# Dense part of a hybrid decoder trunk: weight splits off GpSimd, norm squares after the gains, another order of the first loads

## The chip, the cores and the metric

One NeuronCore of a Trainium2 chip runs the whole program. The metric is device time in microseconds for one execution. The kernel before took 1980.95 us (median of 3 runs, 1980.83 to 1982.15).

## What is computed

A causal decoder trunk of two layers for 256 tokens of width 1024, all in float32. Each layer has a token mixer and then a channel mixer, both behind an RMS norm and both added to the residual stream. The core of the reference:

```python
for layer in range(2):
    h = rms_norm(x, norm_mix_g[layer])
    x = x + hybrid_mixer(h, ...)
    h = rms_norm(x, norm_ffn_g[layer])
    x = x + (swiglu(h, ...) if layer == 0 else moe_swiglu(h, ...))
return rms_norm(x, norm_final_g)
```

The mixer projects h to nine blocks of 1024 columns, runs a gated 3-tap convolution, a GLU with a 31-tap depthwise convolution, layer norm and swish, and a trailing-mean pool over 2, 4, 8 and 16 tokens; it projects the three branches, gates and sums them and projects the sum. Layer 0 has a dense SwiGLU of width 3584, layer 1 a top-2-of-8 mixture of such experts.

## The kernel before, in words

**Matmuls.** Activations lie transposed: channels on the 128 partitions, 256 tokens along the row. A float32 product is made of three fp32r matmuls (`mm3`, L192 to L194): weights and activations are each split into a high part h and a low part l, and the kernel adds h*h, h*l and l*h. A `pair` makes 256 output channels: 8 x 2 weight blocks of 128x128, 48 matmuls, one PSUM bank. In the mixers four banks are used in turn.

**Weights.** `Stream` brings them in chunks of 128x2048 (1 MB, 16 blocks, so one pair for one chunk), in the order of use. `load` (L88) issues the transfers on SyncE's queue, at most four raw buffers deep. `split_upto` makes wh by a ScalarE copy (L112) and wl by a subtraction. The subtraction is one VectorE instruction for a whole chunk (L117). For the chunks listed in `shared`, every odd one of both mixers, VectorE takes the first 1024 columns (L114) and GpSimd the other 1024 (L115). Three split buffers let the splits run ahead of TensorE. The very first chunk is loaded in halves and split in quarters.

**Norm.** The norm's scale is known late, so the first six pairs run on x*gain (`xg`), unscaled, and `descale` multiplies their results by the row of 1/rms. `norm_pair(n, j)` handles 256 channels: two ScalarE copies with the gain (L262), two VectorE instructions for the low part (L263), a ScalarE square (L266, L269) and, for j > 0, a GpSimd add into the sum of squares (L270). `norm_rstd` sums over partitions on TensorE (L228) and takes the inverse root in 12 tiny VectorE instructions (L214 to L220); `norm_row` spreads it over tokens (L236, L241).

**Mixer.** Eight pairs make the GLU, then pool, short convolution (L480, L486), gates and projections. The 31-tap convolution, its layer norm and swish run in the background: a generator emits a few of its instructions at each `bg(k)` call. Its products come from ScalarE (L358) or stay on VectorE (L341), the sums from VectorE (L363). The layer norm adds its squares on GpSimd (L398). The last four gates (L496) and the projection of the result follow it.

**Order.** The instructions of each engine run in one fixed order. It is set when the program is built, by a scheduler that plays the program through on a model of the engines and takes, of what is ready, what was written first; an order can be pinned by hand.

**Head.** SyncE's queue issues, in this order: x's first quarter, prm (gains, 52 KB), weight chunk 0 in two halves, x's other quarters, chunk 1, cst, chunks 2 and 3. ScalarE's queue issues lp (the mixer's parameters, 152 KB).

Of the kernel before, what the change touches and what calls it, by code (L numbers as in the profile page):

```python
# [6 lines left out]
F32 = mybir.dt.float32  # L7
# [8 lines left out]
P = 128  # L16
T = 256
D = 1024
KC = D // P
# [16 lines left out]
N_HL2 = 1  # L36
N_PAD = 4
LEAD = 2
H_POOL = (1, 2, 3)
POOL_ON_DVE = (3,)  # L40

# [7 lines left out]
W2_LATE = E * NFC * 6 - 4  # L49
W2_LATE_AT = {(i, j): (W2_LATE + (j // 2 + 2 if j % 2 else i), HALF * (i if j % 2 else j // 2))  # L50
              for i in range(2) for j in range(4)}


N_MIXER = (72 + 3 * 8 + 8) * KC // (CHUNK // P) + 4 * 4 // (CHUNK // P)
N_FFN = 3 * F // P * KC // (CHUNK // P)
MIXER_CHUNKS = [*range(1, N_MIXER), *range(N_MIXER + N_FFN, 2 * N_MIXER + N_FFN)]


K_ID, K_IOTA, K_INV, K_TRI = 0, 128, 256, 320
# [3 lines left out]
class Act:  # L63


    def __init__(self, h, l):
        self.h, self.l = h, l


class Stream:  # L70


    def __init__(self, nc, srcs, raw, hl, shared):
        self.nc, self.hl, self.shared = nc, [hl] * N_HL, shared
        self.chunks = [s[i] for s in srcs for i in range(s.shape[0])]
        self.n = len(self.chunks)
        self.loaded, self.split, self.pos, self.turn = 0, 0, 0, 0
        self.raws, self.hls = {}, {}
        self.free = [raw] * N_RAW

    def load(self, n=None):

        while self.free and self.loaded < self.n and n != 0:
            c, pool = self.loaded, self.free.pop(0)
            t = pool(f"raw{c}")
            w = HALF if c == 0 else HALF // 2 if c == self.n - 1 else CHUNK
            for o in range(0, CHUNK, w):
                self.nc.sync.dma_start(t[:, o:o + w], self.chunks[c][:, o:o + w])  # L88
            self.raws[c] = (t, pool)
            self.loaded += 1  # L90
            n = n if n is None else n - 1
# [5 lines left out]
    def more_split(self, hl, n):  # L97
        self.hl += [hl] * n

    def split_upto(self, upto):  # L100
        nc = self.nc
        while self.split < min(upto, self.n):
            c = self.split
            t, pool = self.raws.pop(c)
            hl = self.hl[self.turn % len(self.hl)]
            self.turn += 1
            h = hl.tile([P, CHUNK], F32R, tag="wh", name=f"wh{c}")
            l = hl.tile([P, CHUNK], F32R, tag="wl", name=f"wl{c}")
            w = CHUNK // 4 if c == 0 or c == self.n - 1 else HALF if c == self.n - 2 else CHUNK
            for o in range(0, CHUNK, w):  # L110
                d = slice(o, o + w)
                nc.scalar.activation(h[:, d], t[:, d], AF.Copy)  # L112
                if c in self.shared:
                    nc.vector.tensor_tensor(l[:, :HALF], t[:, :HALF], h[:, :HALF].bitcast(F32), ALU.subtract)  # L114
                    nc.gpsimd.tensor_tensor(l[:, HALF:], t[:, HALF:], h[:, HALF:].bitcast(F32), ALU.subtract)  # L115
                else:
                    nc.vector.tensor_tensor(l[:, d], t[:, d], h[:, d].bitcast(F32), ALU.subtract)  # L117
            self.hls[c] = (h, l)
            self.split += 1
            self.free.append(pool)  # L120
            self.load()
# [24 lines left out]
def body(ctx, tc, x_in, prm_in, cst_in, wd_in, wm_in, out):  # L146
# [8 lines left out]
    xT = const.tile([P, KC, T], F32, name="xT")  # L155
    cst = const.tile([P, K_TRI], F32, name="cst")
    prm = const.tile([P, C_END], F32, name="prm")
    ws = Stream(nc, [wd_in, wm_in], lambda name: raw.tile([P, CHUNK], F32, tag="raw", name=name), hlp,
                shared=[c for c in MIXER_CHUNKS if c % 2])

    def load_x(j):
        nc.sync.dma_start(xT[:, 2 * j:2 * j + 2, :], x_in[:, 2 * j:2 * j + 2, :])

    load_x(0)
    nc.sync.dma_start(prm, prm_in[:, 0:C_END])
    ws.load(1)
    for j in range(1, 4):
        load_x(j)
    ws.load(1)
    nc.sync.dma_start(cst, cst_in[:, 0:K_TRI])  # L170
    ws.load()

# [4 lines left out]

    warm = const.tile([P, 1], F32, name="warm")
    nc.scalar.activation(warm, ones[:, 0:1], AF.Sigmoid)

    def col(c, t=prm):
        return t[:, c:c + 1]
# [61 lines left out]
    def new_pair(pool, name):  # L244
        return Act(pool.tile([P, KC, T], F32R, tag="pair", name=f"{name}_h", bufs=6),
                   pool.tile([P, KC, T], F32R, tag="pair", name=f"{name}_l", bufs=6))
# [5 lines left out]
        return n  # L252

    def norm_pair(n, j):
        xp = xT[:, 2 * j:2 * j + 2, :]
        if j == 0:
            n.acc = n.pool.tile([P, 2, T], F32, tag="work", name=f"{n.name}_sqa", bufs=3)
            if n.split:
                n.xg = new_pair(n.pool, f"{n.name}_xg")
        if n.split:  # L260
            for k in (2 * j, 2 * j + 1):
                nc.scalar.activation(n.xg.h[:, k, :], xT[:, k, :], AF.Copy, scale=col(n.g + k))  # L262
                nc.vector.scalar_tensor_tensor(n.xg.l[:, k, :], xT[:, k, :], col(n.g + k),  # L263
                                               n.xg.h[:, k, :].bitcast(F32), ALU.mult, ALU.subtract)
        if j == 0:
            nc.scalar.activation(n.acc, xp, AF.Square)  # L266
        else:
            sq = n.pool.tile([P, 2, T], F32, tag="work", name=f"{n.name}_sq{j}", bufs=3)
            nc.scalar.activation(sq, xp, AF.Square)  # L269
            nc.gpsimd.tensor_tensor(n.acc, n.acc, sq, ALU.add)  # L270
# [33 lines left out]
    def mixer(l, n, dp, on_pair, before_out=lambda: None):  # L304
        with ExitStack() as st:
            mp = st.enter_context(tc.tile_pool(name=f"mix{l}", bufs=1))
            lp = mp.tile([P, M_END], F32, name=f"lp{l}")
            nc.scalar.dma_start(lp, prm_in[:, C_END + l * M_END:C_END + (l + 1) * M_END])
            cvp = st.enter_context(tc.tile_pool(name=f"cvp{l}", bufs=1, space=PSUM))
            mm2 = st.enter_context(tc.tile_pool(name=f"mm2_{l}", bufs=1, space=PSUM))  # L310
            banks[:], turn[0] = [mmp] * 3 + [mm2], 0
# [116 lines left out]
            for j in range(4):  # L428
                s = slice(2 * j, 2 * j + 2)
                ps_v = n.pair(pair)  # L430
                if j == 0:
                    norm_row(n)
                ps_g = n.pair(pair)
                v, g = descale(n, ps_v, 2 * j, tmp), descale(n, ps_g, 2 * j + 1, tmp)
                sg = tmp(f"vsg{l}_{j}")
                nc.scalar.activation(sg, g, AF.Sigmoid)
                nc.vector.tensor_tensor(vg[:, s, CFK - 1:], v, sg, ALU.mult)
                if j == 0:
                    norm_scaled(n)
                else:  # L440
                    bg(8)
# [100 lines left out]
    def ffn(n, dp, nxt):  # L542
        with ExitStack() as st:
            fp = st.enter_context(tc.tile_pool(name="ffn", bufs=1))
            ap = st.enter_context(tc.tile_pool(name="facc", bufs=1, space=PSUM))
            accs = [ap.tile([P, 2, T], F32, name=f"facc{i}") for i in range(4)]
            gs = {}

            def down(fs, js):
                for f, k, m in [(f, k, 2 * j + i) for f in fs for k in range(2) for j in js for i in range(2)]:  # L550
                    wh, wl = ws.take(P)
                    mm3(accs[m // 2][:, m % 2, :], wh, wl, gs[f].h[:, k, :], gs[f].l[:, k, :],
                        start=(f == 0 and k == 0 and m % 2 == 0), stop=(f == NFP - 1 and k == 1))

            def tmp(name):
                return fp.tile([P, 2, T], F32, tag="ft", name=name, bufs=6)

            for f in range(NFP):
                ps_a = n.pair(pair)
                if f == 0:  # L560
                    norm_row(n)
                ps_c = n.pair(pair)
                a, c = descale(n, ps_a, 2 * f, tmp), descale(n, ps_c, 2 * f + 1, tmp)
                sg, t = tmp(f"fsg{f}"), tmp(f"ft{f}")
                nc.scalar.activation(sg, a, AF.Silu)
                nc.vector.tensor_tensor(t, c, sg, ALU.mult)
                gs[f] = Act(fp.tile([P, 2, T], F32R, tag="gh", name=f"gh{f}", bufs=3),
                            fp.tile([P, 2, T], F32R, tag="gl", name=f"gl{f}", bufs=3))
                split2(gs[f], slice(0, 2), t)
                if f == 0:  # L570
                    norm_scaled(n)
                if 1 <= f < NFP - 1:
                    down([f - 1], range(4))
            for j in range(4):
                down([NFP - 2, NFP - 1], [j])
                xp = xT[:, 2 * j:2 * j + 2, :]
                nc.vector.tensor_tensor(xp, accs[j], xp, ALU.add)
                norm_pair(nxt, j)


    class Router:
# [385 lines left out]
    class Final:  # L967
# [24 lines left out]
        def finish(self):  # L992
# [3 lines left out]
            for n, j in enumerate(self.used):  # L996
# [6 lines left out]
    dp = ctx.enter_context(tc.tile_pool(name="dense", bufs=1))  # L1003
    norms = [norm_begin(dp, c, f"n{i}", split=(i < 3)) for i, c in
             enumerate((C_G1[0], C_G2[0], C_G1[1], C_G2[1]))]
    for j in range(4):
        norm_pair(norms[0], j)
    norm_rstd(norms[0])
    mixer(0, norms[0], dp, lambda j: norm_pair(norms[1], j))
    norm_rstd(norms[1])  # L1010
    ffn(norms[1], dp, norms[2])
    norm_rstd(norms[2])
    router = Router(norms[3], dp)
    pools = []

# [140 lines left out]
```

## Time and profile before

| what | value |
|---|---|
| median of 3 runs | 1980.95 us |
| the profiled execution's own time | 1979.97 us |
| its span, first to last instruction | 1978.2 us |
| TensorE busy | 96% of the span, mean granted clock 0.981 |
| VectorE, ScalarE, GpSimd busy | 80%, 65%, 12% |

The profiled execution lies 0.98 us under the median, and 1.77 us of it lie outside the span. TensorE is busy almost throughout, so a change shows in the time where it removes or adds idle time of TensorE, or time at half clock. Times in rows count from the start of the span.

### The profile page before, as it was taken

To read this page: it belongs to the slowest core of one execution; us is meant where nothing else is said; L and a number is where in the kernel's file an instruction comes from. 1 tells how busy PE (TensorE), PEld (TensorE's weight loads), DVE (VectorE), ACT (ScalarE), POOL (GpSimd) and SP (SyncE) were. 2 spreads that over 40 slices of the span, in tenths; PEclk is the share of its full clock that TensorE was granted. 3 is DMA by queue.
4 is the path that set the end of the run, shared out by engine and by line. 5 is a ranking of instruction groups with operands and counts; after the bars stand their busy time and mean duration, and the time that the engine had idled before them with its cause. 6 is when DMAs were issued, how large, how long until landed. Compare 5 with 4: busy or idle time off the path is not lost. (4 is left out here: it accounts for less than half of the span.)

```text
span 1978.2 us, 28849 instructions
## 1 busy us (share of the span) xinstructions
PE 1896.0 (96%) x11819; PEld 1699.4 (86%) x11819; DVE 1588.9 (80%) x1397; ACT 1287.1 (65%) x1301; POOL 245.1 (12%) x135
## 2 busy tenths in 40 slices
PE   8999989999999999978999998999999999999997
PEld 7999989999999999977788886888777888778886
DVE  8999767744469998675888887988878888878886
ACT  6975864533448867654677765776756767667773
POOL 4422342100023423421000000000000000000000
PEclk9999989999999999988999999999999999999998
DMA  7445544554545455445899997999987989879990
GB/s 263 171 171 183 186 165 160 182 185 178 191 155 190 172 192 190 176 174 232 321 375 344 351 337 290 359 366 339 362 307 297 385 328 364 329 283 380 342 361 23
DMA packets 72284, 512.14 MB, mean 259 GB/s; under 512 B 8145, under 2 KB 8657, under 8 KB 10449
## 3 DMA queue, kind: packets, MB, share of 16 engines
q1 hardware_dynamic: 71424, 509.33, 69.2%
q8 instruction: 94, 1.54, 0.3%
q10 hardware_dynamic: 720, 0.90, 0.1%
q14 instruction: 46, 0.37, 0.0%
HBM read 509.15 MB, written 1.05 MB: 258 GB/s over the span
## 5 line engine op out<-in xcount | busy, mean ns | idle before, releaser
L112 ACT ACTIVATE wh<-raw 128x2048 fp32r<-128x2048 f32 (+1 forms) x491 | 925.2, 1892 | 542.2 <-PE mm L193 161.0
L117 DVE TENSOR_TENSOR wl<-raw,wh 128x2048 fp32r<-128x2048 f32 (+1 forms) x438 | 983.6, 2258 | 243.2 <-ACT wh L112 237.0
L192 PE MATMUL mm<-n_h_h,wh 128*128 128x256 f32 x1312 | 372.5, 284 | 4.1 <-DVE cx L480 4.1
L193 PE MATMUL mm<-n_h_l,wh 128*128 128x256 f32 x1312 | 372.1, 284 | 0.0
L194 PE MATMUL mm<-n_h_h,wl 128*128 128x256 f32 x1312 | 372.1, 284 | 0.0
L192 PEld LDWEIGHTS mm<-n_h_h,wh 128*128 128x128 f32 x1312 | 252.8, 193 | 4.4 <-DVE cx L480 4.3
L193 PEld LDWEIGHTS mm<-n_h_l,wh 128*128 128x128 f32 x1312 | 252.8, 193 | 0.0
L194 PEld LDWEIGHTS mm<-n_h_h,wl 128*128 128x128 f32 x1312 | 252.6, 193 | 0.0
L115 POOL TENSOR_TENSOR wl<-raw,wh 128x1024 fp32r<-128x1024 f32 x53 | 149.7, 2824 | 507.6 <-ACT wh L112 500.1
L193 PE MATMUL y<-wl,gt 128*128 128x512 f32 (+1 forms) x464 | 180.7, 392 | 5.2 <-DVE wl L117 5.1
L193 PE MATMUL c<-wl,xe_h 128*128 128x512 f32 x448 | 177.1, 395 | 5.1 <-DVE wl L117 5.1
L193 PE MATMUL a<-wl,xe_h 128*128 128x512 f32 x448 | 178.7, 399 | 3.2 <-DVE wl L117 3.2
L192 PE MATMUL c<-wh,xe_h 128*128 128x512 f32 x448 | 177.1, 395 | 4.9 <-ACT wh L112 4.2
L192 PE MATMUL a<-wh,xe_h 128*128 128x512 f32 x448 | 179.5, 402 | 0.0
L194 PE MATMUL y<-wh,gt 128*128 128x512 f32 (+1 forms) x464 | 178.8, 391 | 0.4 <-DVE gt L871 0.4
L194 PE MATMUL a<-wh,xe_l 128*128 128x512 f32 x448 | 176.8, 396 | 0.0
L194 PE MATMUL c<-wh,xe_l 128*128 128x512 f32 x448 | 176.1, 393 | 0.0
L192 PE MATMUL y<-wh,gt 128*128 128x512 f32 (+1 forms) x464 | 169.7, 391 | 4.9 <-ACT wh L112 4.9
L358 ACT ACTIVATE cvp<-vg,lp 128x256 f32<-128x256 f32 x360 | 153.1, 498 | 20.9 <-DVE cvw L363 19.8
L363 DVE TENSOR_TENSOR cvw<-cvw,cvp 128x1024 f32<-128x1024 f32 (+1 forms) x116 | 110.9, 956 | 3.5 <-ACT cvp L358 1.4
L193 PEld LDWEIGHTS y<-wl,gt 128*128 128x128 f32 x464 | 88.1, 190 | 25.7 <-DVE wl L117 6.9
L192 PEld LDWEIGHTS y<-wh,gt 128*128 128x128 f32 x464 | 88.0, 190 | 24.5 <-ACT wh L112 5.6
(242 smaller groups left out, 3236.3 us busy)
## 6 DMA issues: line engine op xcount, KB each, us to landing
raw<-wm_dram SPq DMA_DIRECT2D x335, 1024.0 KB, 6.7
raw<-wd_dram SPq DMA_DIRECT2D x147, 1024.0 KB, 4.9
xT<-x_dram SPq DMA_DIRECT2D x4, 256.0 KB, 6.8
raw<-wd_dram SPq DMA_DIRECT2D x2, 512.0 KB, 5.8
raw<-wm_dram SPq DMA_DIRECT2D x4, 256.0 KB, 6.3
out_dram<-o SPq DMA_DIRECT2D x2, 256.0 KB, 2.4
out_dram<-o ACTq DMA_DIRECT2D x2, 256.0 KB, 2.4
lp<-prm_dram ACTq DMA_DIRECT2D x2, 152.0 KB, 3.4
```

Source lines behind the costliest of these rows:

```text
L112: nc.scalar.activation(h[:, d], t[:, d], AF.Copy)
L115: nc.gpsimd.tensor_tensor(l[:, HALF:], t[:, HALF:], h[:, HALF:].bitcast(F32), ALU.subtract)
L117: nc.vector.tensor_tensor(l[:, d], t[:, d], h[:, d].bitcast(F32), ALU.subtract)
L192: nc.tensor.matmul(ps, lh, rh, start=start, stop=False, skip_group_check=True)
L193: nc.tensor.matmul(ps, lh, rl, start=False, stop=False, skip_group_check=True)
L194: nc.tensor.matmul(ps, ll, rh, start=False, stop=stop, skip_group_check=True)
L358: nc.scalar.activation(pr[:, i, :], src, AF.Copy, scale=w)
L363: nc.vector.tensor_tensor(dst, acc_c, pr, ALU.add)
```

## The change

Six edits, in the dense part and the head:

1. `shared` goes: every low part of a weight is made by VectorE alone, in one instruction.
2. x comes in one transfer on SyncE's queue; prm goes to ScalarE's queue; chunk 1 too is loaded and split in halves; the mixer's lp in layer 0 goes to SyncE's queue, behind the first chunks.
3. 14 float32 matmuls of a 128x128 block of ones run at the start of TensorE's program; nobody reads them.
4. The first chunk's quarters are pinned: gain copies of pair j, low parts of pair j, split of quarter j, for j = 0 to 3.
5. The squares of the first norm are issued behind the last quarter's copy on ScalarE; those of the norm between the layers come after the gains of all four pairs.
6. `norm_rstd` of the two mixer norms is written after the mixer's first pair, `norm_row` after its second.

```diff
+N_BUSY = 14
...
-            w = HALF if c == 0 else HALF // 2 if c == self.n - 1 else CHUNK
+            w = HALF if c < 2 else HALF // 2 if c == self.n - 1 else CHUNK
...
-            w = CHUNK // 4 if c == 0 or c == self.n - 1 else HALF if c == self.n - 2 else CHUNK
+            w = CHUNK // 4 if c in (0, self.n - 1) else HALF if c in (1, self.n - 2) else CHUNK
             for o in range(0, CHUNK, w):
                 d = slice(o, o + w)
-                nc.scalar.activation(h[:, d], t[:, d], AF.Copy)
-                if c in self.shared:
-                    nc.vector.tensor_tensor(l[:, :HALF], t[:, :HALF], h[:, :HALF].bitcast(F32), ALU.subtract)
-                    nc.gpsimd.tensor_tensor(l[:, HALF:], t[:, HALF:], h[:, HALF:].bitcast(F32), ALU.subtract)
-                else:
-                    nc.vector.tensor_tensor(l[:, d], t[:, d], h[:, d].bitcast(F32), ALU.subtract)
+                first(o // w)
+                self.last = keep(nc.scalar.activation(h[:, d], t[:, d], AF.Copy))
+                keep(nc.vector.tensor_tensor(l[:, d], t[:, d], h[:, d].bitcast(F32), ALU.subtract))
...
-    load_x(0)
-    nc.sync.dma_start(prm, prm_in[:, 0:C_END])
-    ws.load(1)
-    for j in range(1, 4):
-        load_x(j)
-    ws.load(1)
+    nc.scalar.dma_start(prm, prm_in[:, 0:C_END])
+    nc.sync.dma_start(xT, x_in)
+    ws.load(2)
     nc.sync.dma_start(cst, cst_in[:, 0:K_TRI])
...
+    busy = stp.tile([P, P], F32, tag="st", name="busy")
+    for _ in range(N_BUSY):
+        tc.keep_in_program_order(nc.tensor.matmul(busy, ones, ones, start=True, stop=True))
...
-            nc.scalar.dma_start(lp, prm_in[:, C_END + l * M_END:C_END + (l + 1) * M_END])
+            (nc.scalar if l else nc.sync).dma_start(lp, prm_in[:, C_END + l * M_END:C_END + (l + 1) * M_END])
...
                 ps_v = n.pair(pair)
                 if j == 0:
+                    norm_rstd(n)
+                ps_g = n.pair(pair)
+                if j == 0:
                     norm_row(n)
-                ps_g = n.pair(pair)
...
                 nc.vector.tensor_tensor(xp, accs[j], xp, ALU.add)
-                norm_pair(nxt, j)
+                norm_gain(nxt, j)
+            for j in range(4):
+                norm_square(nxt, j)
...
-    for j in range(4):
-        norm_pair(norms[0], j)
-    norm_rstd(norms[0])
+    keep = tc.keep_in_program_order
+    ws.split_upto(1, lambda q: norm_gain(norms[0], q, keep), keep)
+    with tc.issue_after(ws.last.ins):
+        for j in range(4):
+            norm_square(norms[0], j)
     mixer(0, norms[0], dp, lambda j: norm_pair(norms[1], j))
     norm_rstd(norms[1])
     ffn(norms[1], dp, norms[2])
-    norm_rstd(norms[2])
```

`norm_gain` and `norm_square` are the two halves of `norm_pair`, with the same instructions.

## Rows read from the trace of the kernel before

**Rows 1.** Waits of TensorE (line waited for: us in total, times, longest)

```profile
PE mm L192 <- ACT g L496: 16.8, 2, 8.8
PE mm L192 <- ACT wh L112: 7.8, 1, 7.8
...
PE mm L192 <- DVE cx L480: 4.1, 1, 4.1
...
PE mm L193 <- DVE n_xg_l L263: 2.6, 4, 1.5
...
PE ln_row L236 <- DVE ln_y L220: 1.4, 1, 1.4
PE n_sum L228 <- DVE n_sqa L225: 1.3, 1, 1.3
PE mm L194 <- DVE wl L117: 1.2, 1, 1.2
```

**Rows 2.** Windows: us, busy (instructions) of PE, PEld, DVE, ACT, POOL, granted clock, DMA

```profile
121.40:128.20 6.80, 4.59 (x21) 4.59 (x22) 6.80 (x10) 5.20 (x10) 0.25 (x2) 0.50 0.53 194
...
285.20:295.50 10.30, 5.02 (x22) 4.78 (x23) 7.39 (x8) 9.78 (x17) 3.39 (x1) 0.50 0.30 102
...
7.70:12.10 4.40, 4.33 (x19) 4.11 (x20) 4.20 (x7) 4.29 (x11) 1.20 (x1) 1.00 1.05 399
...
19.00:22.40 3.40, 3.37 (x15) 3.07 (x15) 3.12 (x10) 1.81 (x1) 1.51 (x1) 0.50 0.74 246
22.40:30.00 7.60, 7.60 (x66) 7.60 (x65) 6.17 (x7) 2.30 (x2) 0.86 (x1) 1.00 0.58 212
...
851.80:862.10 10.30, 4.91 (x23) 4.91 (x24) 4.48 (x8) 10.30 (x22) 0.43 (x2) 0.50 0.48 196
```

**Rows 3.** Timeline (start, us, engine, line): the head, and one row of the end

```profile
7.08 2.41 ACT L112 ACTIVATE wh<-raw 128x512 fp32r<-128x512 f32 x4 [0.41 <-DMA raw<-wd_dram]
...
10.72 0.90 ACT L262 ACTIVATE n_xg_h<-xT,prm 128x256 fp32r<-128x256 f32 x2
...
11.52 0.61 ACT L269 ACTIVATE n_sq<-xT 128x512 f32<-128x512 f32 x1
...
1970.15 1.22 PE L236 MATMUL fin_row<-cst,fin_y 128*128 128x128 f32 x4 [2.42 <-DVE fin_y L220]
```

**Rows 4.** VectorE's groups from 30 to 124 us (count, busy us, mean ns)

```profile
L114 DVE TENSOR_TENSOR wl<-raw,wh 128x1024 fp32r<-128x1024 f32 x8 | 16.1, 2013 | 0.0
...
L486 DVE SCALAR_TENSOR_TENSOR c<-cx,lp,c 128x256 f32<-128x256 f32 x4 | 3.8, 994 | 0.0
...
L457 DVE TENSOR_TENSOR us<-us 128x514 f32<-128x514 f32 x1 | 2.3, 2327 | 0.0
...
L457 DVE TENSOR_TENSOR us<-u 128x542 f32<-128x542 f32 x1 | 2.0, 1981 | 0.0
...
L457 DVE TENSOR_TENSOR us<-us 128x538 f32<-128x538 f32 x1 | 0.7, 705 | 0.0
```

**Rows 5.** Line 114, whole span (duration ns min/median/max)

```profile
L114 DVE TENSOR_TENSOR wl<-raw,wh x53: 1206/1227/3465, 18.2 to 887.5; 128x1024 fp32r<-128x1024 f32 x53
```

**Rows 6.** Timeline of VectorE and GpSimd, 113 to 122 us

```profile
113.75 0.87 DVE L486 SCALAR_TENSOR_TENSOR c<-cx,lp,c 128x256 f32<-128x256 f32 x2
...
118.87 2.96 DVE L486 SCALAR_TENSOR_TENSOR c<-cx,lp,c 128x256 f32<-128x256 f32 x2
...
119.05 2.50 POOL L115 TENSOR_TENSOR wl<-raw,wh 128x1024 fp32r<-128x1024 f32 x1 [2.54 <-ACT wh L112]
```

**Rows 7.** Timeline of VectorE and GpSimd, 260 to 273 us

```profile
266.21 2.29 DVE L117 TENSOR_TENSOR wl<-raw,wh 128x2048 fp32r<-128x2048 f32 x1 [2.21 <-ACT wh L112]
...
272.22 3.28 DVE L114 TENSOR_TENSOR wl<-raw,wh 128x1024 fp32r<-128x1024 f32 x1
...
260.50 2.42 POOL L115 TENSOR_TENSOR wl<-raw,wh 128x1024 fp32r<-128x1024 f32 x1 [8.44 <-ACT wh L112]
...
265.12 5.71 POOL L398 TENSOR_TENSOR vsum<-vsum,lsq 128x512 f32<-128x512 f32 x3
```

**Rows 8.** Timeline of VectorE, 584 to 591 us

```profile
584.07 6.88 DVE L263 SCALAR_TENSOR_TENSOR n_xg_l<-xT,prm,n_xg_h 128x256 fp32r<-128x256 f32 x4
```

More of the change, by code (lines that the diff above doesn't have):

```diff
@@ L51 @@
               for i in range(2) for j in range(4)}
-N_MIXER = (72 + 3 * 8 + 8) * KC // (CHUNK // P) + 4 * 4 // (CHUNK // P)
-N_FFN = 3 * F // P * KC // (CHUNK // P)
-MIXER_CHUNKS = [*range(1, N_MIXER), *range(N_MIXER + N_FFN, 2 * N_MIXER + N_FFN)]
 K_ID, K_IOTA, K_INV, K_TRI = 0, 128, 256, 320
@@ L70, with __init__ @@
 class Stream:
-    def __init__(self, nc, srcs, raw, hl, shared):
-        self.nc, self.hl, self.shared = nc, [hl] * N_HL, shared
+    def __init__(self, nc, srcs, raw, hl):
+        self.nc, self.hl = nc, [hl] * N_HL
         self.chunks = [s[i] for s in srcs for i in range(s.shape[0])]
@@ L98, in more_split, with split_upto @@
         self.hl += [hl] * n
-    def split_upto(self, upto):
+    def split_upto(self, upto, first=lambda q: None, keep=lambda ins: ins):
         nc = self.nc
@@ L157, in body @@
     prm = const.tile([P, C_END], F32, name="prm")
[L158 to L162, printed above, removed]
-    load_x(0)
-    nc.sync.dma_start(prm, prm_in[:, 0:C_END])
-    ws.load(1)
-    for j in range(1, 4):
-        load_x(j)
-    ws.load(1)
+    ws = Stream(nc, [wd_in, wm_in], lambda name: raw.tile([P, CHUNK], F32, tag="raw", name=name), hlp)
+    nc.scalar.dma_start(prm, prm_in[:, 0:C_END])
+    nc.sync.dma_start(xT, x_in)
+    ws.load(2)
     nc.sync.dma_start(cst, cst_in[:, 0:K_TRI])
@@ L254, in norm_pair, with norm_gain, norm_square @@
     def norm_pair(n, j):
+        norm_gain(n, j)
+        norm_square(n, j)
+    def norm_gain(n, j, keep=lambda ins: ins):
+        if not n.split:
+            return
+        if j == 0:
+            n.xg = new_pair(n.pool, f"{n.name}_xg")
+        for k in (2 * j, 2 * j + 1):
+            keep(nc.scalar.activation(n.xg.h[:, k, :], xT[:, k, :], AF.Copy, scale=col(n.g + k)))
+            keep(nc.vector.scalar_tensor_tensor(n.xg.l[:, k, :], xT[:, k, :], col(n.g + k),
+                                                n.xg.h[:, k, :].bitcast(F32), ALU.mult, ALU.subtract))
+    def norm_square(n, j):
         xp = xT[:, 2 * j:2 * j + 2, :]
@@ L257, in norm_pair @@
             n.acc = n.pool.tile([P, 2, T], F32, tag="work", name=f"{n.name}_sqa", bufs=3)
[L258 to L265, printed above, removed]
             nc.scalar.activation(n.acc, xp, AF.Square)
@@ L431, in mixer @@
                 if j == 0:
+                    norm_rstd(n)
+                ps_g = n.pair(pair)
+                if j == 0:
                     norm_row(n)
-                ps_g = n.pair(pair)
                 v, g = descale(n, ps_v, 2 * j, tmp), descale(n, ps_g, 2 * j + 1, tmp)
```

## Prediction, made before the change was run

> **What bounds the kernel now.** TensorE is busy nearly all the time, so I first read what it waited for [rows 1]. Seven entries matter: 7.8 us before the first matmul; in the head and at the norm between the layers n_xg_l (four waits, 2.6 us), wl (1.2) and n_sum (1.3); 4.1 us for cx in layer 0's mixer; and, at the end of each mixer, a gate's ScalarE copy (16.8 us in two waits, the longer 8.8, so the other 8.0), with 1.4 us for ln_row. Then I read windows [rows 2], to see what such a wait costs afterwards. From 22.4 us on 66 matmuls start in 7.6 us, 0.12 us each: the engine's full rate. After the cx wait the granted clock is 0.50 for 6.8 us, after each mixer's last wait for 10.3 us; at that level (1.2 of 2.4 GHz) half of a stretch is lost: 3.4 us and twice 5.1 us. So cx stands for 4.1 + 3.4 = 7.5 us, the first mixer's end for 8.0 + 5.1 = 13.1, the second's for 1.4 + 8.8 + 5.1 = 15.3. The time can fall only where these do. The last thing read was why VectorE is late there: its groups, then it and GpSimd side by side [rows 4 to 7].
>
> **No weight splits on GpSimd.** Removed are 53 half splits on GpSimd; VectorE's 53 halves become whole. A half takes 1.21 us when nothing hinders it [rows 5], a whole 2.29 [rows 7], so each costs VectorE 1.08 us. What it gives back: while GpSimd runs a split of 2.50 us, two VectorE instructions that took 0.87 us earlier take 2.96 [rows 6]. From 30 to 124 us, where VectorE has hardly a pause and the cx wait arises, there are 8 halves: 8 x 1.08 = 8.6 us added. Given back [rows 4]: the halves themselves, 8 x (2.01 - 1.21) = 6.4; two of L457, (2.33 + 1.98) - 2 x 0.70 = 2.9; L486, 4 x 0.99 less 2 x 0.87 = 2.2 [rows 4, 6]. That is 11.5, a net relief of 2.9 us, and 0 if a part was due to other GpSimd work; blocked instructions not counted here could make it 5. The cx wait of 4.1 us therefore shrinks to about 1 or goes; a wait of that size (ln_row's 1.4, say) is not one of those followed by half clock in rows 2. **Gain 6 us** of the 7.5; what is late next is ScalarE's copies for the same convolution.
>
> **Ends of the mixers.** The last gates and the projection wait for the layer norm's chain: GpSimd's sum of squares, the inverse root, swish. In the chain of layer 0 a split (2.42 us from 260.50) stands ahead of the three squares' adds, which take 5.71 us [rows 7]; it goes. Then a half of 3.28 us stands before the inverse root; as a whole without GpSimd beside it, it takes 2.29: 1.0 saved. The chain is thus up to 3.4 us shorter. Against this, ScalarE's order (two weight copies and the swish ahead of the gates) is unchanged, and a whole split late in the chain costs 1.1 more. Bounds: 1 us worse, or all 13.1 gone. I take 3 us of wait and about 1 us of half clock: **4 us**. The second mixer's end shows the same wait in rows 1, so the same **4 us**, ln_row's wait among them.
>
> **Norm between the layers.** Four L263, 0.45 us each where nothing hinders them, took 6.88 us beside GpSimd's adds of squares [rows 8]. With gains first, squares and adds come later. The waits there are two of n_xg_l, 2.0 us, and wl, 1.2 [rows 1]. The first go; the second shrinks by a square ahead of its copy, 0.61 less overlap [rows 3], some 0.5. **Gain 2.5 us**, bounds 0 and 3.2. The later squares delay norm_row, but four PSUM banks give TensorE two more pairs, over 11 us, before it needs a bank. Writing norm_rstd and norm_row one pair later costs nothing under the same cover.
>
> **Head.** Lost so far after the first matmul: from 7.7 to 12.1 us 19 matmuls start in 4.4 us; at 0.12 each that is 2.1 us lost. Waits: 0.6 (n_xg_l, the other 2.0 of its 2.6 being the later norm's) and 1.3 (n_sum). Half clock from 19.0 to 22.4: 15 matmuls in 3.4 us, 1.6 lost [rows 1, 2]. Sum 5.6. Lost afterwards: ahead of the first half chunk go 52 + 1024 KB, where 256 + 52 + 152 KB went: 616 KB more, at the 399 GB/s of that window [rows 2] 1.6 us, though longer rows of x may save some; 1.4. The halves of chunk 0 land at about 8.5 and 9.8 us instead of 7.1 [rows 3]. Each quarter takes ScalarE 0.90 + 0.60 us against TensorE's 12 x 0.12 = 1.44: 0.2 in all. Then four squares, 4 x 0.61 = 2.4 us [rows 3], stand ahead of chunk 1's first half copy, about 1.0; the last quarter gives TensorE some 2.1 us of cover: 1.3 idle, and 0.9 for the half's low part. Half clock after that: nothing or 1.6, 0.8 taken. Sum 4.6. **Gain 1 us**, bounds -1.5 (adds of squares hold the low part) and 4 (x lands fast, or the copy goes ahead of the squares).
>
> The 14 matmuls of ones are not in the trace. The nearest row is two float32 products of this size in four pieces, 1.22 us at half clock [rows 3]: 14 x 0.61 = 8.5 us as the upper bound, 14 x 0.305 = 4.3 (the same at full clock) as the lower. They need only the ones, so I start them at 1 us; they end between 5.3 and 9.5. I take 7, at half clock first and full later, and so nothing on the path. If they end early, the idle time behind them may bring half clock back; that is the lower bound above. lp now queues on SyncE behind the chunks, and behind the wait for a free raw buffer; it is needed only with the first tap, tens of microseconds later: nothing. prm takes lp's slot on ScalarE's queue: nothing.
>
> **Sum.** 6 + 4 + 4 + 2.5 + 1 = 17.5 us. The profiled execution, 1979.97 us, would become 1962.5; the median lies 1.0 above it: 1963.5, say 1963.
>
> **Rivals.**
>
> *VectorE becomes the bound.* If what blocked it was GpSimd's other work (adds, pooling), nothing comes back, and the 8.6 us add to the cx wait: 12.7 us, with 10.3 us at half clock instead of 6.8, 1.7 more. That is +10.3; less 3.5 from head and norm, 1988 us. It decides once the relief per split is under 1.08 us. For it: VectorE has no slack there. Against it: 11.5 us over 8 splits are 1.4 each, and rows 6 show the blocking beside a split. Chance 0.10.
>
> *GpSimd's chain is held instead.* Rows 6 show one engine waiting for the whole of the other's instruction; it works both ways, since three adds took 5.71 us [rows 7], 1.9 each. Whole splits of 2.29 us would hold the remaining adds of squares as the half splits of GpSimd delayed them, and the mixers' ends keep their waits: no gain of 4 + 4, perhaps 1 us lost; 1980.95 - 9.5 + 1 = 1972.5. Chance 0.17. The Trainium skill's page "SBUF — State Buffer", section "Who interferes with whom", states this: a VectorE instruction with two SBUF inputs and a GpSimd instruction that reads SBUF exclude one another, and whichever starts first keeps the port for all of its length. By that rule the longer VectorE instruction is the worse holder. The rows agree on the blocking; none shows a whole split holding an add in the chain.
>
> *The order undoes it.* The scheduler's new order keeps the late cx and the late gates: only 3.5 us from head and norm remain, 1977.5, or none. Chance 0.07.
>
> **Numbers.** The forecast has 0.66, its own range 1950 to 1972: the mixers' ends each from 1 worse to 9 better, the head from -1.5 to 4, cx 4 to 7.5. The range for 8 in 10 takes in the second rival and the edge of the third: 1948 to 1977. Outside 0.2%, 4 us, which is about what a measurement of this kernel can tell from no change: faster 0.83 (the forecast and the second rival), within it 0.07, slower 0.10.
>
> **What would show it.** Right: L114 and L115 are gone; L117 takes 2.29 us throughout, L486 0.47; the wait for cx is under 1.5 us and no half clock stands near 120 us; the waits for L496 sum to 8 to 13 us instead of 16.8; n_xg_l leaves the list at the second norm. In the head the first matmul of a weight starts near 9.2 us at full clock, and TensorE's next idle time is before chunk 1. Wrong: a cx wait over 4 us (first rival), L398 still over 1.9 us on average and L496 still at 16 us (second), or the head reaching chunk 2 later than before.

## The result and the profile after the change

The changed kernel is **slower**, by 1.4%: 2009.2 us (median of 4 runs, 2007.83 to 2013.51) against 1981.48 (4 runs of the kernel before beside it), ratio 1.0142, 95% interval 1.013 to 1.0154. The profiled execution took 2008.27 us, its span 2006.4. The prediction was 1963 us, range 1948 to 1977.

First the waits of TensorE in the changed kernel (line waited for: us in total, times, longest), against [rows 1].

```profile
PE mu L382 <- DVE sums L380: 17.5, 2, 9.7
PE mm L183 <- ACT g L495: 14.5, 2, 7.3
PE ln_sum L219 <- DVE vsum L216: 14.0, 2, 7.0
...
PE ln_row L227 <- DVE ln_y L211: 5.0, 2, 2.5
...
PE mm L185 <- DVE wl L111: 3.7, 4, 1.2
```

The cx wait of 4.1 us and the n_xg_l waits are gone, as forecast. But mu and ln_sum, which did not wait before, now wait 17.5 and 14.0 us, twice each: the layer norm at the end of both mixers. Its first wait is for `sums`, the sum over channels that closes the 31-tap convolution.

To see where the time came from, the first of the three matmuls of every weight block was numbered, and its start compared with that of the same number before:

| place | start before, us | after less before, us |
|---|---|---|
| first weight matmul | 7.8 | +0.8 |
| chunk 1 | 18.8 | -2.7 |
| behind the cx wait, chunk 18 | 127.6 | -9.1 |
| last gates, first mixer | 279.1 | -9.5 |
| first mixer's last projection | 290.5 | +10.4 |
| second norm | 589.9 | +8.3 |
| second mixer's last projection | 857.2 | +27.0 |
| end | 1978.2 | +28.2 |

So the change won 9.5 us up to the last gates, and lost 19.9 and 18.7 us at the two mixers' ends. Of the 9.5 us, 1.3 are only put off: the matmuls of mu, ln_sum and ln_row, which the kernel before had run by then. A new wait of 0.95 us for a whole split's wl, at 175 us, had taken 1.2 us back. The timeline of TensorE shows the first end (start us, us, engine, line; in brackets the idle time before and its releaser).

```profile
280.70 1.22 PE L382 MATMUL mu<-sums,ones 128*128 128x256 f32 x2 [7.74 <-DVE sums L380]
288.93 1.01 PE L219 MATMUL ln_sum<-ones,vsum 128*128 128x1 f32 x4 [7.01 <-DVE vsum L216]
292.46 1.19 PE L227 MATMUL ln_row<-cst,ln_y 128*128 128x128 f32 x4 [2.52 <-DVE ln_y L211]
300.91 0.58 PE L183 MATMUL mm<-v_h,wh 128*128 128x256 f32 x1 [7.26 <-ACT g L495]
```

The whole chain from `sums` to the projection's first operand runs with no gate left beside it: 24.5 us idle (7.74 + 7.01 + 2.52 + 7.26), where the kernel before idled 8.0. The windows say what the clock adds and how the stretches compare (us, busy (instructions) of PE, PEld, DVE, ACT, POOL, granted clock, DMA), against [rows 2].

```profile
8.70:12.10 3.40, 3.35 (x15) 3.06 (x16) 3.40 (x8) 3.40 (x9) 0.00 (x0) 0.51 1.05 419
...
52.00:175.40 123.40, 122.55 (x1022) 122.35 (x1020) 115.82 (x129) 98.36 (x163) 13.76 (x16) 1.00 0.49 171
...
210.50:279.40 68.90, 62.46 (x521) 62.25 (x519) 51.68 (x48) 47.55 (x74) 6.48 (x5) 0.97 0.52 183
275.00:305.70 30.70, 8.22 (x32) 7.15 (x33) 15.97 (x32) 16.36 (x35) 3.85 (x3) 0.50 0.11 39
858.70:889.40 30.70, 8.62 (x34) 7.55 (x35) 15.29 (x34) 17.05 (x35) 4.29 (x5) 0.50 0.19 71
```

Half clock now lasts 30.7 us at each end, where it lasted 10.3. Only work that is done at half clock loses time: half of the 8.22 us of PE, 4.1, against half of 5.02, 2.5 [rows 2]. First end: 24.5 - 8.0 in waits and 4.1 - 2.5 in clock are 18.1 of the 19.9 us; the matmuls put off make it 19.4. Second end: 26.5 idle (9.72 + 7.01 + 2.52 + 7.26) less 10.2, and 4.3 - 2.5: 18.1 of 18.7.

**Why `sums` is late.** The line that closes the convolution, in the kernel before and then in the changed one (duration ns min/median/max, then first and last start: one per mixer).

```profile
L383 DVE TENSOR_TENSOR sums<-sums x2: 424/425/426, 252.8 to 822.6; 128x256 f32<-128x256 f32 x2
```
```profile
L380 DVE TENSOR_TENSOR sums<-sums x2: 425/426/426, 280.2 to 863.5; 128x256 f32<-128x256 f32 x2
```

It starts 27.4 us later, though the matmuls beside it are 8.2 us earlier. The convolution works on eight groups of 128 channels, numbered 0 to 7. VectorE's wide adds for groups 0 to 3 end 15.5 us later (their last starts at 175.36, before at 159.90); up to there VectorE is busy 115.8 of 123.4 us, so added work delays them. The last adds, for groups 6 and 7, take 12.4 us longer: from 214.4 to its end at 279.4, before from 199.5 to 252.1. Two chunks of this last stretch on VectorE, first before, then after:

```profile
225.42 1.32 DVE L114 TENSOR_TENSOR wl<-raw,wh 128x1024 fp32r<-128x1024 f32 x1 [0.53 <-ACT wh L112]
226.66 1.49 DVE L363 TENSOR_TENSOR cvw<-cvw,cvp 128x512 f32<-128x512 f32 x2
228.33 1.50 DVE L363 TENSOR_TENSOR cvw<-cvw,cvp 128x512 f32<-128x512 f32 x2 [0.17 <-ACT cvp L358]
231.23 2.29 DVE L117 TENSOR_TENSOR wl<-raw,wh 128x2048 fp32r<-128x2048 f32 x1 [1.40 <-ACT wh L112]
233.44 1.50 DVE L363 TENSOR_TENSOR cvw<-cvw,cvp 128x512 f32<-128x512 f32 x2
...
235.72 0.69 DVE L363 TENSOR_TENSOR cvw<-cvw,cvp 128x512 f32<-128x512 f32 x1
```
```profile
240.26 2.40 DVE L111 TENSOR_TENSOR wl<-raw,wh 128x2048 fp32r<-128x2048 f32 x1 [0.53 <-ACT wh L110]
242.58 1.49 DVE L360 TENSOR_TENSOR cvw<-cvw,cvp 128x512 f32<-128x512 f32 x2
244.25 0.70 DVE L360 TENSOR_TENSOR cvw<-cvw,cvp 128x512 f32<-128x512 f32 x1 [0.17 <-ACT cvp L355]
246.05 2.29 DVE L111 TENSOR_TENSOR wl<-raw,wh 128x2048 fp32r<-128x2048 f32 x1 [1.10 <-ACT wh L110]
248.26 0.69 DVE L360 TENSOR_TENSOR cvw<-cvw,cvp 128x512 f32<-128x512 f32 x1
...
250.57 0.69 DVE L360 TENSOR_TENSOR cvw<-cvw,cvp 128x512 f32<-128x512 f32 x1
```

Each shows 11.5 us, two chunks. Before, seven adds of the convolution fit between the splits; now five. The split that was half grew from 1.32 to 2.40 us. VectorE still pauses (1.10 for wh), but no add could fill this pause. The one after it, at 248.26, needs products that ScalarE makes only from 246.40 on, behind the weight copy for which the split waits too:

```profile
243.30 0.91 ACT L355 ACTIVATE cvp<-vg,lp 128x256 f32<-128x256 f32 x2 [1.47 <-DVE cvw L360]
244.12 1.90 ACT L110 ACTIVATE wh<-raw 128x2048 fp32r<-128x2048 f32 x1
...
246.40 1.70 ACT L355 ACTIVATE cvp<-vg,lp 128x256 f32<-128x256 f32 x4
```

Of the twelve pauses before a split in this stretch (12.6 us together), none had the next add's operands ready. ScalarE in turn had waited 1.47 us for VectorE's add, which stood behind the split of 2.40 us, to free one of the two product buffers. So here the longer split does not only use VectorE's time: it also holds the products back.

### The profile page after: what moved, and what is told of

It reads as the page before. It is cut to its first block, busy times and chain, and to the rows that moved or that the text cites. A ratio compares the mean times of both kernels' runs of the same rounds, so it can differ in the third digit from the quotient of the medians.

```text
span 2006.4 us, 28788 instructions
## 1 busy us (share of the span) xinstructions
PE 1900.8 (95%) x11847; PEld 1703.4 (85%) x11847; DVE 1583.9 (79%) x1398; ACT 1286.1 (64%) x1302; POOL 94.0 (5%) x82
## 5 line engine op out<-in xcount | busy, mean ns | idle before, releaser
L111 DVE TENSOR_TENSOR wl<-raw,wh 128x2048 fp32r<-128x2048 f32 (+1 forms) x492 | 1112.7, 2273 | 269.4 <-ACT wh L110 266.7
L183 PEld LDWEIGHTS y<-wh,gt 128*128 128x128 f32 x464 | 88.0, 190 | 24.5 <-ACT wh L110 5.6
L184 PEld LDWEIGHTS c<-wl,xe_h 128*128 128x128 f32 x448 | 84.6, 189 | 26.7 <-DVE wl L111 8.9
```

What stands on the lines that cost most here:

```text
L111: keep(nc.vector.tensor_tensor(l[:, d], t[:, d], h[:, d].bitcast(F32), ALU.subtract))
L183: nc.tensor.matmul(ps, lh, rh, start=start, stop=False, skip_group_check=True)
L184: nc.tensor.matmul(ps, lh, rl, start=False, stop=False, skip_group_check=True)
```

## The experiments

The theory after the result: whole splits take from VectorE the time in which it did the background convolution; this ends behind the last gates, and the layer norm's chain is exposed. Rivals: GpSimd's part of the chain is at fault, or the new order of norm and head. Runs with a ratio and an interval are medians of four or five executions; the others are single ones. Edits are against the changed kernel unless said otherwise.

**Splits back.** The split by halves returns for all odd mixer chunks but the first.

```diff
+SHARED = [c for c in MIXER_CHUNKS if c % 2 and c > 1]
...
+                if c in SHARED:
+                    nc.vector.tensor_tensor(l[:, :HALF], t[:, :HALF], h[:, :HALF].bitcast(F32), ALU.subtract)
+                    nc.gpsimd.tensor_tensor(l[:, HALF:], t[:, HALF:], h[:, HALF:].bitcast(F32), ALU.subtract)
+                    continue
```

> The changed kernel with the GpSimd half splits put back for the odd mixer chunks from 3 on; all other edits stay. Theory A (the longer VectorE splits make the background convolution late, so that the layer norm's sum mu comes after the last gates): mu's wait on VectorE goes, both mixer ends return to about the waits of before (8 to 9 us and 10 us of half clock each), the gain of the head (2.7 us) and of the second norm (2 us) stay, the cx wait returns at least in part: 1970 to 1978 us. Theory B (the other edits, above all the later norm_rstd and norm_row, start the convolution late): no change, about 2008 us.

Measured: 1974.39 us, ratio 0.9959 (0.9944 to 0.9973). `sums` is back at 250.3 us and the ends wait as before, 8.03 and 1.44 + 8.79 us. The head is 3.7 us ahead by chunk 1, but a half clock from 18.0 us on leaves 0.7 of this by chunk 18; of the cx wait 1.98 us are left; the n_xg_l waits at the second norm are back (1.52 and 0.45).

**The kernel before, without splits on GpSimd** (an edit to the kernel before).

```diff
-                shared=[c for c in MIXER_CHUNKS if c % 2])
+                shared=[])
```

> The kernel before with an empty list of shared chunks; nothing else changed. Theory A: the cx wait goes (6 us gained) and each mixer end loses 15 to 20 us: 2005 to 2016 us. Theory B: only the gain of the cx wait, 1973 to 1976 us.

Measured: 2007.64 us (1999.35 to 2008.45), ratio 1.0114 (1.009 to 1.0138). Its waits of TensorE:

```profile
PE mm L192 <- ACT g L496: 14.5, 2, 7.3
PE ln_sum L228 <- DVE vsum L225: 14.0, 2, 7.0
PE mu L385 <- DVE sums L383: 13.8, 2, 7.7
...
PE ln_row L236 <- DVE ln_y L220: 5.0, 2, 2.5
```

The same four waits, with the old head and the old order of the norm: the splits alone make the loss. The cx gain (6.2 us) and the second norm's (2.2) come with them too, so the second comes from the splits and not from putting the squares last. Even 1.9 us in the head come with them, by chunk 18.

**A shorter convolution**, twice. First 10 of 31 taps are left out for groups 6 and 7 (the last stretch), then 15 of 31 for groups 4 and 5, which VectorE makes alone, long before the end. (The expectations say 11 and 16, but the last tap stays, so each edit leaves out one fewer, and the second 30 instructions of VectorE, not 32.)

```diff
-                    for k in range(CFK):
+                    for k in (range(CFK) if n > 2 else [*range(CFK - 11), CFK - 1]):
```

> The changed kernel with 11 of the 31 taps left out for the last two groups of 128 channels of the convolution (another result for 256 of its channels); all splits stay on VectorE. Theory A: what counts is when the convolution ends against the last gate; 11 rounds at 2.8 rounds per chunk bring mu forward by 4 chunks (22 us), its wait goes, and the two mixer ends fall back to 8 to 13 us of idle time in all each: 1965 to 1980 us. Rival (the chain behind mu is itself longer without GpSimd's halves, whenever it starts): the waits for ln_sum, ln_row and v stay as long, and only mu's own 8 to 10 us go: about 1990 us.

Measured: 1970.02 us. `sums` comes at 257.3 us; of the four waits only ln_row's 1.46 and the projection's 8.78 are left at each end, as at the second end of the kernel before.

```diff
-                    for k in range(CFK):
+                    for k in [*range(CFK - 16), CFK - 1]:
```

> The changed kernel with 16 of the 31 taps left out for the two groups of 128 channels whose taps VectorE makes alone (another result for 256 channels): 32 instructions of about 0.4 us, 13 us of VectorE work less ahead of the last group; all splits stay on VectorE. Leftover theory (the convolution gets what the splits and the foreground leave of VectorE, about 2.5 us per chunk, so 13 us of work are about 5 chunks, 25 to 30 us of its end): the waits for mu and ln_sum go, 1966 to 1976 us. Rival (a microsecond of work is a microsecond of delay): mu comes only 13 us earlier, some waits stay, 1982 to 1992 us.

Measured: 1964.05 us. The line of `sums` in this kernel:

```profile
L380 DVE TENSOR_TENSOR sums<-sums x2: 416/416/417, 251.0 to 812.5; 128x256 f32<-128x256 f32 x2
```

It is 29 us earlier, and mu, ln_sum and ln_row no longer wait. Work taken from VectorE early in the mixer, about 13 us by the expectation's estimate, brings the end forward by more than twice as much: the convolution lives on what VectorE leaves over, long before its last stretch.

**Splits in one part of the mixer**: the first experiment with another list of chunks, early (odd chunks 3 to 27) and late (29 to 41).

```diff
-SHARED = [c for c in MIXER_CHUNKS if c % 2 and c > 1]
+SHARED = [c for c in MIXER_CHUNKS if c % 2 and 1 < c % (N_MIXER + N_FFN) < 28]
```

> The changed kernel with GpSimd's half splits only for the odd chunks 3 to 27 of each mixer, where VectorE has hardly a pause, and none in the later part of the convolution or its layer norm. If the late start of the last convolution group is what costs (VectorE load before it), it comes back: mixer ends as before, 1970 to 1980 us. If the slower rounds of that last group cost as much (2.8 rounds per chunk instead of 3.4, about 13 us), half of the loss stays: 1988 to 1998 us.

```diff
-SHARED = [c for c in MIXER_CHUNKS if c % 2 and c > 1]
+SHARED = [c for c in MIXER_CHUNKS if c % 2 and 28 < c % (N_MIXER + N_FFN) < 42]
```

> The changed kernel with GpSimd's half splits only for the odd chunks 29 to 41 of each mixer, the counterpart of e8_splits_early. If the two stretches simply add up (e8 gave back 20 of 34 us against e1_splits_back), this one gives back about 14 us: 1992 to 1998 us, with the last convolution group starting near 214 us as in the changed kernel. If the last group's rounds are what counts, it gives back more than half: under 1990 us.

Measured: 1988.14 and 1985.05 us. Of the 34.8 us between the changed kernel and the one with all splits back, early splits bring back 21.1 and late ones 24.2, each more than half; the two do not add up. Early, a cx wait of 1.99 us is back; late, the gains at cx and at the second norm stay (9.2 us by the last gates, 2.2 at the norm).

**No splits at the very end** (the first experiment's list without chunks 43, 45 and 47 of each mixer), for the forecast term that GpSimd's splits lengthen the chain.

```diff
-SHARED = [c for c in MIXER_CHUNKS if c % 2 and c > 1]
+SHARED = [c for c in MIXER_CHUNKS if c % 2 and c > 1 and not 40 < (c - 1) % (N_MIXER + N_FFN) < 47]
```

> As e1_splits_back, but no GpSimd split for the chunks 43, 45 and 47 of each mixer, the ones beside the layer norm's chain. The prediction's term (the chain gets 3.4 us shorter without the splits in it): each mixer end loses 3 us of wait and up to 3 us of half clock, 1974 - 10 = 1964 us. Rival (the chain is paced by ScalarE's fixed order and by the chunks, and a whole split on VectorE costs what GpSimd's half cost): within 3 us of e1_splits_back, 1972 to 1977 us.

Measured: 1975.03 us, ratio 0.996 (0.9946 to 0.9974), as with them. The first end still waits 8.29 us, and the three adds of squares on GpSimd still take 5.67: one of them takes 3.12 us, beside a whole split on VectorE.

```profile
L405 POOL TENSOR_TENSOR vsum<-vsum,lsq x6: 1189/1194/3124, 261.0 to 831.3; 128x512 f32<-128x512 f32 x6
```

At the second end ln_row's wait goes and the other is 7.27 instead of 8.79. Measured by the start of the second mixer's last projection, this kernel is 5.4 us ahead of the one with the splits back, of which 1.9 were there at the second norm, so this end won 3.5 us. None of the 5.4 us is left at the kernel's end: with nearly the same waits, TensorE runs 37.5 us at half clock in the expert stage (the mixture of layer 1) behind that projection, and in the kernel with the splits back 23.9. One stretch of it, first splits back, then this kernel:

```profile
1190.00:1260.00 70.00, 63.48 (x282) 50.97 (x281) 58.02 (x44) 45.66 (x34) 0.00 (x0) 0.98 0.80 299
```
```profile
1190.00:1260.00 70.00, 63.47 (x271) 50.86 (x270) 55.70 (x43) 42.85 (x32) 0.00 (x0) 0.93 0.77 295
```

**A third product buffer** for the convolution, and 20 matmuls of ones instead of 14; first on the kernel of the last experiment, then on the changed kernel without any split on GpSimd, then with splits in odd chunks 19 to 41.

```diff
-N_BUSY = 14
+N_BUSY = 20
...
-                            pr = mp.tile([P, 4, T], F32, tag="cvpr", name=f"cvp{l}_{j}_{k}", bufs=2)[:, 0:n, :]
+                            pr = mp.tile([P, 4, T], F32, tag="cvpr", name=f"cvp{l}_{j}_{k}", bufs=3)[:, 0:n, :]
```

> As e4_tail_without, with three buffers instead of two for the convolution's products and 20 instead of 14 matmuls of ones. Theory A (the time hangs on where the convolution's end stands against the last gates): the order has the sum mu about one chunk earlier, so the waits at the mixer ends shrink by 3 to 6 us each and the half clock with them; the ones bridge the 2.1 us of idle time before the first weight matmul, so its chunk runs at full clock, 1 to 2 us: 1955 to 1965 us. Rival: the ends are held by ScalarE's own 8 us of swish and gates, and nothing moves but the head, 1971 to 1974 us.

Measured: **1966.94 us** (1965.23 to 1968.76), ratio 0.9922 (0.9906 to 0.9939), the best of those that make every tap, and better than both kernels. Its waits of TensorE from 100 to 320 us:

```profile
PE mm L193 <- ACT g L505: 3.1, 1, 3.1
PE mm L193 <- DVE cx L489: 2.0, 1, 2.0
```

Against the kernel of the last experiment it is 1.3 us ahead by chunk 18 (the ones) and 6.2 behind the first end (the buffer too). There `sums` is ready only 1.6 us earlier, but mu's matmul starts 5.3 us earlier (248.2 against 253.5): it has a fixed place in TensorE's order, and that place moved.

> The changed kernel with three product buffers (cvpr) instead of two and 20 matmuls of ones instead of 14, no splits on GpSimd. The written order is the same at the convolution's end (mu at place 2164 of TensorE's order, as without the third buffer). Theory (the order of VectorE's work is fixed when the kernel is built, and a third buffer gives VectorE no more time): four waits at each mixer's end of 20 us or more together, as in the changed kernel; only the head changes: no half clock between the ones and the 19th matmul, 1 to 2 us won; total 2005 to 2009. Rival (VectorE's adds wait for ScalarE's products, so the lack of a buffer makes the convolution late): the end waits shrink by 5 us or more each, total under 1998.

Measured: 2000.84 us (one run), between the two expectations. The waits of TensorE from 100 to 320 us:

```profile
PE ln_sum L219 <- DVE vsum L216: 8.8, 1, 8.8
PE mm L183 <- ACT g L495: 7.3, 1, 7.3
PE ln_row L227 <- DVE ln_y L211: 2.5, 1, 2.5
PE mu L382 <- DVE sums L380: 1.1, 1, 1.1
```

A buffer brings `sums` forward by 5.9 us and takes most of mu's wait, part of which ln_sum gets back. So VectorE's adds are also held by the buffers of ScalarE's products, which the theory had denied; it remains the smaller part, since 19.7 us of waits stay where the kernel before had 8.0.

> The changed kernel with the shared splits back for the odd mixer chunks 19 to 41 only, three product buffers (cvpr) instead of two, and 20 matmuls of ones instead of 14. Theory (what VectorE leaves for the convolution decides): the early chunks stay without GpSimd's splits, so the cx wait stays under 1.5 us and about 9 us are won by chunk 19; from there the halves give VectorE back about 0.5 us a chunk, so mu stands at place 2042 of TensorE's fixed order instead of 2164 (the fast version with splits nearly throughout: 1929), and each mixer's end costs 0 to 6 us instead of 19; the second norm keeps its 2 us. Total 1964 to 1972 us. Rival (the splits hurt wherever they stand beside the convolution, and only their removal everywhere or nowhere pays): above 1975, with a wait at the mixers' ends as in the changed kernel.

Measured: 1971.4 us (1970.94 to 1972.86), ratio 0.9953 (0.9937 to 0.997). It keeps the gain at cx (9.2 us by chunk 18) and at the second norm, but waits 0.4 + 9.8 us at each end, more than the kernel above, and loses to it.

In the order in which `sums` is ready, the idle time at the first end grows too, with two small exceptions. The kernel's time follows it less closely. It also holds what was won or lost elsewhere, among it the half clock of the expert stage: from the second mixer's last projection to the end, the kernels differ from the one before by 2.4 us less to 4.4 us more.

| kernel | `sums` in the first mixer, us | idle at its end, us | second mixer's last projection, less before, us | time, us |
|---|---|---|---|---|
| three buffers, splits but at the end | 247.8 | 3.1 | -10.0 | 1966.94 |
| splits but at the end | 249.4 | 8.3 | -7.0 | 1975.03 |
| splits back | 250.3 | 8.0 | -1.6 | 1974.39 |
| kernel before | 252.8 | 8.0 | 0 | 1981.48 |
| three buffers, splits 19 to 41 | 253.6 | 10.2 | -7.2 | 1971.4 |
| splits late | 262.8 | 14.2 | +5.3 | 1985.05 |
| splits early | 264.6 | 13.6 | +5.3 | 1988.14 |
| three buffers, no splits | 274.3 | 19.7 | +16.4 | 2000.84 |
| kernel before, no splits | 280.1 | 22.8 | +25.2 | 2007.64 |
| changed kernel | 280.2 | 24.5 | +27.0 | 2009.2 |

## Why the prediction was wrong

**No weight splits on GpSimd: right.** The step gave a gain of 6 us at cx; measured 6.4 (from -2.7 to -9.1). The blocking was real: line 486 had taken up to 2.56 us for one instruction, and its successor never takes over 0.49.

```profile
L486 DVE SCALAR_TENSOR_TENSOR c<-cx,lp,c x32: 466/472/2564, 113.7 to 733.2; 128x256 f32<-128x256 f32 x32
```
```profile
L485 DVE SCALAR_TENSOR_TENSOR c<-cx,lp,c x32: 472/478/487, 108.8 to 738.3; 128x256 f32<-128x256 f32 x32
```

The whole wait and its clock were worth less than the 7.5 us put down for them: half clock takes half of the 4.59 us of work in that window [rows 2], 2.3, not half of the window. 4.1 + 2.3 is 6.4, all of which came. The remark that a wait of 1.4 us is not followed by half clock misread the rows: n_sum's wait of 1.3 us ended at 18.4 us, and half clock stood from 19.0 [rows 2]. With the splits back, the 1.98 us left of the cx wait were followed by 3.4 us of it. Here it did not matter, as the wait went whole.

**Ends of the mixers: the step that failed.** The text had "4 us" of gain at each end, with 1 us worse as the bad bound; they lost 19.9 and 18.7. It counted a split inside the layer norm's chain, and asked nowhere when that chain starts. Where it asked what is late next, it answered "ScalarE's copies for the same convolution"; what came late was the end of the 31-tap convolution, which has no place of its own in TensorE's work and takes what VectorE leaves. The 1.08 us added per odd chunk were set against the relief only up to 124 us, where the cx wait arises. Beyond it the adds go on to 252 us, and they have no relief at all: their durations are the same with GpSimd's splits beside them and without, first before, then after:

```profile
L363 DVE TENSOR_TENSOR cvw<-cvw,cvp x116: 679/957/1233, 50.1 to 815.8; 128x1024 f32<-128x1024 f32 x58, 128x512 f32<-128x512 f32 x58
```
```profile
L360 DVE TENSOR_TENSOR cvw<-cvw,cvp x116: 685/958/1232, 52.3 to 861.2; 128x1024 f32<-128x1024 f32 x58, 128x512 f32<-128x512 f32 x58
```

These adds keep their sum `cvw` in PSUM (so does `cva`, 491 ns at most in both kernels). The Trainium skill's page "SBUF — State Buffer", section "Who interferes with whom", cited in the prediction for its other half, states this too: a VectorE instruction with at most one input in SBUF does not contend with GpSimd outside certain modes. The rows agree. Had it been applied to each group of the trace, the relief of 11.5 us per 8 splits would not have stood for the whole mixer.

The term "up to 3.4 us shorter" for the chain can have come at one end of two at most, and only with the convolution in time: without splits at the end the second mixer's end won 3.5 us (its `sums` came 1.7 us earlier too), but the first waits as long as before (8.29 us).

**Norm between the layers: the size right, the cause wrong.** 2.5 us were forecast, 2.2 measured (from +10.2 ahead of it to +8.0 behind it). The n_xg_l waits go wherever no split of the second mixer's first chunks runs on GpSimd, and stay wherever one does, squares last or not. The part of wl (0.5) did not come: it waits 1.2 us in every kernel.

**Head: the sign right, undersized.** 1 us was forecast, 2.7 measured by chunk 1. The first matmul comes at 8.58 us (9.2), the ones end at 6.4 (7), and 2.1 idle us behind them bring half clock from 8.7 to 12.1: the case named as the lower bound. But 15 matmuls then run without a pause, and of the later waits only wl's 0.9 us is left where n_sum, n_xg_l and the half clock at 19.0 stood. Most of this is not the head's edits: the kernel before without splits on GpSimd has the old head and is 1.9 us ahead by chunk 18, the changed kernel 2.9. In the kernel before, chunk 1's split on GpSimd had held the add for which n_sum waits; without splits it takes 0.41 us. First both rows before, then without splits:

```profile
15.43 2.60 POOL L115 TENSOR_TENSOR wl<-raw,wh 128x1024 fp32r<-128x1024 f32 x1 [0.32 <-ACT wh L112]
15.71 2.60 DVE L225 TENSOR_TENSOR n_sqa<-n_sqa 128x256 f32<-128x256 f32 x1
```
```profile
16.21 0.41 DVE L225 TENSOR_TENSOR n_sqa<-n_sqa 128x256 f32<-128x256 f32 x1
```

**Rivals.** *VectorE becomes the bound* named the right engine and sign, but put it at cx with 10.3 us, and its point of decision (relief under 1.08 us per split) was not met there: the cx wait went. *GpSimd's chain is held* did not cause the loss: in the changed kernel the three adds of squares take 4.01 us, before 5.71 [rows 7]. But its mechanism is real, and the prediction was wrong that no row showed it. In rows 7 the whole split L117 (from 266.21, 2.29 us) ran beside the adds, and one of them took 3.17 us instead of 1.19:

```profile
L398 POOL TENSOR_TENSOR vsum<-vsum,lsq x6: 1192/1198/3169, 265.1 to 835.5; 128x512 f32<-128x512 f32 x6
```

The same is seen without splits at the end (3.12 us). In the changed kernel the adds come so late that no split runs beside them. *The order undoes it* fell too. The three terms that came, 6.4 + 2.2 + 2.7, are 11.3 us, more than the 9.5 forecast for them; the two ends alone turn this into a loss.

What stays open: how the delay in the convolution's last stretch divides between VectorE's time, the two product buffers and ScalarE's order, in which products stand behind weight copies that still wait; the third buffer (with 20 ones, without splits) brought 5.9 of 27.4 us. Whether another order by hand would keep all gains was not tried.

## What to carry to other kernels

When work moves onto an engine that also carries a background task, work out when that task ends, from the time the engine has left per step over the whole stage and from what its operands wait for, and not only from what happens at the wait that is to go. A relief counts only for the instructions that were blocked: check it group by group, for operands in PSUM apart from those in SBUF. Give the offload back where the background is being worked off, and leave it out where the blocked instructions stand.

## What the runs showed of the hardware that was not expected

**Half clock follows the idle, at little price of its own.** With the idle time at a mixer's end growing from 3.1 over 8.0 to 24.5 us, the stretch at 0.50 grew from 6.8 over 10.2 to 30.7 us; yet of those 30.7 only the 8.2 us of work in it cost anything, 4.1 us.

**The head's half clock moved without a plain rule.** Behind the ones, 2.14 us of idle brought it at once (8.7 us); with 2.72 us idle in the kernel with splits back it came only at 18.0, behind a wait of 1.84 for wl; with 20 ones, 0.56 us idle and the same wait of 1.84 (splits 19 to 41) none came in the head at all.

**Half clock far behind the edits.** Leaving out the half clock at the second mixer's end and that of the last 25 us, the time at 0.50 in the expert stage is 23.9, 30.7 or 37.5 us, depending on the kernel: 30.7 in the kernel before and the changed one, 23.9 with the splits back, 37.5 without splits at the end. From the second mixer's last projection to the end, the kernels with 23.9 took 0.6 to 2.4 us less than the kernel before, and those with 37.5 took 2.9 to 4.4 more, though no edit touches the expert stage. A difference of a few us between two kernels' times is therefore better read place by place.
